# Products of normed rows from layer 1 on as fp16 pairs, with a scale measured for each weight matrix

## The chip, the cores and the metric

One core of a Trainium2 chip runs the whole program. The metric is the device time of one execution in microseconds. The 3 executions of the kernel before took 3876.66 to 3880.73 us, with a median of 3877.01 us.

## What is computed

Two blocks of two layers each work on 512 rows ("latent" tokens) of 1024 features; in the first block 256 context rows go along. Cut to what matters:

```python
# first block, layers l = 0, 1 (context rows get an output in layer 0 only)
u  = modulate(rms_norm(h, g_norm1[l]), shift1, scale1)       # "normed rows"
p  = u @ w_in[l]                 # 1024 x 2720: queries, keys, values of three attentions
g  = sigmoid(u @ w_gate[l] + b_gate[l])                      # 1024 x 3072
h  = h + m2 * (sum(g * (ys @ w_branch[l])) @ w_o[l])
u2 = modulate(rms_norm(h, g_norm2[l]), shift2, scale2)
h  = h + m5 * ((silu(gate) * val) @ w_down[l])               # gate, val = dwconv(u2 @ w_up[l]), 1024 x 5632
# second block, layers l = 0, 1
p  = rmsnorm(x, attn_norm_w[l]) @ w_in_2[l]                  # 1024 x 2964: SSD, short conv, sparse attention
x  = x + concat(y_ssd, y_sc, y_nsa) @ w_out_2[l]
x  = x + (silu(gate) * val) @ ffn_w_down_2[l]                # gate, val = dwconv(rmsnorm(x, .) @ ffn_w_up_2[l]), 1024 x 5504
```

Everything is float32 in memory. The kernel makes each float32 product from two-part operands: with hi = the rounded value and lo = the rest, it adds hi·hi, hi·lo and lo·hi.

## The kernel before

Features lie on the 128 partitions, so a row block of 1024 features is 8 tiles of 128 x 512 (latent) and 8 of 128 x 256 (context). A product with 128 columns of a weight matrix is `mm3`: for each of the 8 feature tiles `wh·uh` and `wh·ul`, then for each `wl·uh`, 24 products into one PSUM bank, each with its own weight load. Both parts of both operands are float32r tiles (4 bytes). `Norm.scale` writes the two parts of the normed rows (`uh`, `ul`: 16 buffers of tag U); `WS.get` loads a block of weights of 256 columns (SyncE's queue, 2 buffers of tag wr) and splits 128 columns of it at a time: ScalarE writes `wh` (128 x 1024), VectorE, or GpSimd where `g.wpool` is set, writes `wl`; 3 buffers each.

The stages follow each other: first block layer 0 (mixer, FFN), layer 1 (mixer, FFN), second block layer 0 and layer 1 (mixer, FFN each). The mixers weave score, softmax and value steps of the heads with products of `w_in`, `w_gate` and others as filling (`weave`, `Fill`). `ffn` goes in chunks of 4 tiles of 128 inner columns: `up` makes gate and value tiles (two products of 24, each evicted by `conv_tile`: one ScalarE and two VectorE instructions that read PSUM), `down` adds the chunk's product to all 8 tiles of `h` (12 products each, evicted by VectorE). During the FFN the generator `ahead` prepares the next layer's parameters. `consumer` is the norm at the end of the FFN: it runs tile by tile behind the last `down`.

The program is written in Tile: a scheduler sets the order on each engine by the order of the program and a model of durations, and hands out buffers of a tag as they come free; engines then run their queues in order. `issue_after(x)` puts an instruction behind `x` on x's engine. K is the tag of wide work tiles: 14 of them in the first block, 22 in the second. PSUM has 8 banks, handed out by tags pM, pT, po, pS; `g.banks` is the list from which `dense` takes its bank in turn. In the second block's mixers it is `["pM"]` (2 banks), and `g.wpool = 1` sends every `wl` of these mixers to GpSimd.

Of the kernel before, what the change touches and what calls it, by code (L numbers as in the profile page):

```python
# [14 lines left out]
OP = mybir.AluOpType  # L15
# [50 lines left out]
class Gen:  # L66
    def __init__(self, tc, ins, outs, ctx, dbg=None):
# [4 lines left out]
        self.hold = []  # L72
# [55 lines left out]
    def parts(self, n, name):  # L128
# [4 lines left out]
        return out  # L133

# [134 lines left out]

    def stats(self, sq, Dn, ntt, eps=EPS, bank="po", small=False):  # L270
# [100 lines left out]
    def dense_raw(self, wp, x, segs, M=P, r0=0, tag="R"):  # L371
        out = self.slot(tag, "dr")
        for sg in segs:
            ps = yield from self.dense(wp, x, sg, M)
            self.act(out[r0:r0 + M, sg[0]:sg[0] + sg[1]], ps)
        return out
# [81 lines left out]
class Norm:  # L458
    def __init__(self, g, h, n, A, B, parts=THIRDS):
        self.g, self.h, self.n, self.A, self.B = g, h, n, A, B  # L460
        self.u, self.rp, self.acc, self.sq = None, [], {}, {}
        self.tiles = [x for x in parts if x[0] < n]

# [59 lines left out]
    def scale(self, i, ks=range(KD)):  # L523
        g = self.g
        o, w = self.tiles[i]
        if self.u is None:
            self.u = [g.parts(self.n, "u") for _ in self.h]
        rp = self.cols(i)
        for k in ks:
# [40 lines left out]
class Between(Norm):  # L570
    def __init__(self, g, h, g1, f):
# [4 lines left out]
        self.A = [gw]  # L576
        self.rs = g.param([P, 4], name="rsk")
# [74 lines left out]
class WS:  # L652
# [7 lines left out]
    def get(self, c, M):  # L660
# [30 lines left out]
        out.key = (id(self), c)  # L691
        return out
# [235 lines left out]
class First:  # L928
    def __init__(self, g, l, h, ada_next=None):
# [4 lines left out]
        self.nq = T if self.ctxq else S  # L934

# [71 lines left out]
    def win(self, c0, c1, cc=256):  # L1007
        return self.g.wstream(self.g.I["w_in"][self.l], 0, KD, c0, c1, cc)
# [329 lines left out]
    def gates(self):  # L1338
        g = self.g
        wg = g.wstream(g.I["w_gate"][self.l], 0, KD, 0, 3 * D)  # L1340
        self.th = []

        def one(d):
            th = g.slot("L", "th")
            wt = wg.get(d * P, P)
            for o, wd in self.qsegs:
                ps = yield from g.dense(wt, self.u, (o, wd))
                g.act(th[:, o:o + wd], ps, AF.Tanh, scale=0.5, bias=self.hbg[:, d:d + 1])
# [73 lines left out]
    def project(self, merged, sp):  # L1422
# [19 lines left out]
        return h, Norm(g, h, nq, A, B).run(tile, self.qsegs)  # L1442

    def run(self, ahead, consumer):
# [16 lines left out]
        u = ffn(g, u2, h, self.qsegs, I["w_up"][l], I["w_down"][l], D_FF, self.cw, self.cb, (0, 44 // 2), 1,  # L1461
# [6 lines left out]
def conv_tile(g, ps, seg, out, cw, cb, c, lead, M):  # L1468
    o, w = seg
    nt = len(cw)  # L1470
    g.act(out[:M, o:o + w], ps, AF.Identity, scale=cw[lead][:M, c:c + 1], bias=cb[:M, c:c + 1])
    for j in range(nt):
# [5 lines left out]
        g.stt(x, ps[:, a + d:b + d], cw[j][:M, c:c + 1], x, OP.mult, OP.add)  # L1478


def ffn(g, u, h, segs, w_up, w_down, dff, cw, cb, coff, lead, scale, consumer, ahead):
# [3 lines left out]
    wg = g.wstream(w_up, 0, KD, 0, dff)  # L1485
    wv = g.wstream(w_up, 0, KD, dff, 2 * dff)
# [3 lines left out]
    def up(ts):  # L1490
        hs = []
        for p0 in range(0, len(ts), 2):
            pair = ts[p0:p0 + 2]
            gates = []
            for t in pair:
# [3 lines left out]
                for sg in segs:  # L1499
                    conv_tile(g, drain(g.dense(w, u, sg, M)), sg, x, cw, cb, coff[0] + t, lead, M)  # L1500
                g.act(x[:M, :n], x[:M, :n], AF.Silu)
                gates.append(x)
            for t, gt in zip(pair, gates):
# [27 lines left out]
    def rest(c, hs):  # L1531
        tile = down(c, hs)
        for d in range(KD):
            for sg in segs:
                tile(d, sg)
    for c in cs[:-2]:
# [3 lines left out]
    drain(ahead)  # L1540
    out = consumer(h).run(down(cs[-1], b), segs, SPLIT)
# [4 lines left out]
class Second:  # L1546
    def __init__(self, g, l, h):
        self.g, self.l, self.h = g, l, h
        self.ws = {}
# [37 lines left out]
    def win(self, c0, c1):  # L1587
        if (c0, c1) not in self.ws:
            self.ws[c0, c1] = self.g.wstream(self.g.I["w_in_2"][self.l], 0, KD, c0, c1, P)
        return self.ws[c0, c1]  # L1590

    def begin(self):
# [3 lines left out]
        hi, lo = g.t("wh", [P, KD, 44], F32R, "wh"), g.t("wl", [P, KD, 44], F32R, "wl")  # L1596
# [3 lines left out]
        g.split(hi, lo, raw)  # L1600
# [634 lines left out]
```

## Time and profile before

| | us |
|---|---|
| median of 3 executions | 3877.01 |
| the profiled execution, device time | 3866.76 |
| its span, first to last instruction | 3865.0 |
| TensorE busy in it | 3704.6 (96%) |
| VectorE, ScalarE, GpSimd busy | 2458.5, 1794.8, 512.0 |

The stages as the loads of their weights bound them in the trace: first block layer 0 mixer 0 to 822, FFN 822 to 1400; layer 1 mixer 1400 to 2075, FFN 2075 to 2455; second block layer 0 mixer 2455 to 2775, FFN 2775 to 3148; layer 1 mixer 3148 to 3462, FFN 3462 to 3865. A product's busy time holds the way through the array, and neighbours overlap; what counts is the distance of their starts. A row of the timeline that merges x products gives it: the start of the next row less its own start, through x; or, with a length L, (L - one duration) / (x - 1).

### The profile page before, as it was taken

Reading aid. Unit: us, or ns where it says so; the run is one execution under the profiler, and the core shown is the slowest. Engines: PE = TensorE matmul, PEld = TensorE weight load, DVE = VectorE, ACT = ScalarE, POOL = GpSimd, SP = SyncE. Lnnn points to the kernel's source line nnn. Section 1 sums busy time; section 2 is a strip of 40 time slices with the busy share of each in tenths; the row PEclk is TensorE's granted clock in tenths of the full one; section 3 lists DMA queues with packets and bytes.
Section 4 is the critical chain, followed back from the end, with each engine's and each line's share of the span. In section 5 each row is a group of like instructions: output and inputs, shape, how many; then the busy total and the mean of one; then the engine's idle time right before and its main releaser. Section 6 shows DMA issues by size and latency. Waiting matters only on the chain. (4 is left out here: it accounts for less than half of the span.)

```text
span 3865.0 us, 54467 instructions
## 1 busy us (share of the span) xinstructions
PE 3704.6 (96%) x20896; PEld 3078.4 (80%) x20896; DVE 2458.5 (64%) x4270; ACT 1794.8 (46%) x3000; POOL 512.0 (13%) x423
## 2 busy tenths in 40 slices
PE   8999999999999999989999999989999998999999
PEld 6888887888888888867767888767788876778886
DVE  5857676656544467668665555678765567876555
ACT  4646666424333236557654333455543335554333
POOL 2101110221000003121112000234100003410000
PEclk9999999999999999999999999989999998999999
DMA  8636898922222225559993322324433322453231
GB/s 246 145 90 153 180 218 226 244 89 79 88 77 87 72 77 131 118 136 216 232 274 126 110 95 93 94 70 104 113 100 98 96 83 67 99 132 98 88 106 60
DMA packets 692255, 483.96 MB, mean 125 GB/s; under 512 B 345790, under 2 KB 620892, under 8 KB 691996
## 3 DMA queue, kind: packets, MB, share of 16 engines
q1 hardware_dynamic: 686172, 468.33, 45.5%
q0 software_dynamic: 5824, 12.15, 1.6%
q8 instruction: 165, 2.70, 0.3%
q14 instruction: 94, 0.77, 0.1%
HBM read 339.32 MB, written 38.67 MB: 98 GB/s over the span
## 5 line engine op out<-in xcount | busy, mean ns | idle before, releaser
L176 ACT ACTIVATE wh<-w 128x1024 fp32r<-128x1024 f32 (+5 forms) x518 | 503.1, 975 | 720.3 <-PE pM L189 232.3
L179 DVE TENSOR_TENSOR wl<-w,wh 128x1024 fp32r<-128x1024 f32 (+3 forms) x464 | 526.0, 1136 | 359.8 <-ACT wh L176 99.7
L189 PE MATMUL pM<-uh,wh 128*128 128x512 f32 (+5 forms) x1832 | 687.2, 381 | 14.6 <-ACT dr L176 9.4
L189 PE MATMUL pM<-ul,wh 128*128 128x512 f32 (+5 forms) x1832 | 662.4, 375 | 0.0
L189 PE MATMUL pM<-uh,wl 128*128 128x512 f32 (+5 forms) x1832 | 450.0, 373 | 0.0
L189 PEld LDWEIGHTS pM<-uh,wh 128*128 128x128 f32 (+3 forms) x1832 | 352.3, 192 | 79.3 <-ACT dr L176 12.7
L189 PEld LDWEIGHTS pM<-ul,wh 128*128 128x128 f32 (+3 forms) x1832 | 343.4, 191 | 56.7
L189 PEld LDWEIGHTS pM<-uh,wl 128*128 128x128 f32 (+3 forms) x1832 | 327.2, 189 | 56.7
L189 PE MATMUL pT<-uh,wh 128*128 128x512 f32 (+3 forms) x912 | 311.1, 353 | 3.0 <-ACT uh L176 2.3
L189 PE MATMUL pT<-ul,wh 128*128 128x512 f32 (+3 forms) x912 | 298.2, 348 | 0.0
L176 ACT ACTIVATE p<-pS,nb 128x768 f32<-128x768 f32 (+7 forms) x304 | 217.6, 716 | 122.4 <-DVE nb L793 116.8
L793 DVE TENSOR_REDUCE nb<-pS 128x1 f32<-128x768 f32 (+7 forms) x304 | 218.0, 725 | 54.6 <-PE pS L189 52.9
L182 DVE SCALAR_TENSOR_TENSOR hl<-p,sm,hl 128x768 f16<-128x768 f32 (+5 forms) x224 | 174.2, 781 | 71.9 <-ACT hl L176 70.4
L176 ACT ACTIVATE hl<-p,sm 128x768 f16<-128x768 f32 (+5 forms) x224 | 159.9, 719 | 108.5 <-DVE sm L1297 26.2
L185 POOL TENSOR_TENSOR rs<-st,half 128x2 f32<-128x2 f32 (+2 forms) x34 | 32.3, 949 | 1327.8 <-DVE st L512 1148.9
L189 PE MATMUL pT<-uh,wl 128*128 128x512 f32 (+3 forms) x912 | 205.3, 351 | 0.0
L185 POOL TENSOR_TENSOR wl<-w,wh 128x1024 fp32r<-128x1024 f32 (+1 forms) x54 | 129.6, 2404 | 537.6 <-ACT wh L176 421.6
L189 PEld LDWEIGHTS pT<-uh,wh 128*128 128x128 f32 (+2 forms) x912 | 171.4, 188 | 28.8 <-ACT uh L176 4.3
L189 PE MATMUL po<-pt,v 128*128 128x128 f16 (+1 forms) x1656 | 174.8, 250 | 16.6 <-DMA pt<-hl 13.0
L189 PEld LDWEIGHTS pT<-ul,wh 128*128 128x128 f32 (+2 forms) x912 | 166.7, 186 | 22.5
L189 PEld LDWEIGHTS <-v 128*128 128x128 f16 x1656 | 123.3, 101 | 60.9 <-issue 43.8
L189 PEld LDWEIGHTS pT<-uh,wl 128*128 128x128 f32 (+2 forms) x912 | 153.8, 188 | 21.9 <-issue 0.4
(581 smaller groups left out, 7763.0 us busy)
## 6 DMA issues: line engine op xcount, KB each, us to landing
w<-w_up SPq DMA_DIRECT2D x44, 1024.0 KB
aw<-w_ada SPq DMA_DIRECT2D x40, 1024.0 KB
w<-ffn_w_up SPq DMA_DIRECT2D x40, 1024.0 KB
w<-w_in SPq DMA_DIRECT2D x70, 512.0 KB
w<-w_gate SPq DMA_DIRECT2D x24, 1024.0 KB
w<-w_down SPq DMA_DIRECT2D x20, 1024.0 KB
ld<-spill SPq DMA_DIRECT2D x51, 384.0 KB
w<-ffn_w_down SPq DMA_DIRECT2D x16, 1024.0 KB
```

Of the source, the lines that this page charges most:

```text
L176: return self.nc.scalar.activation(out, in_, func, **kw)
L179: return self.nc.vector.tensor_tensor(out, a, b, op=op)
L182: return self.nc.vector.scalar_tensor_tensor(out, a, s, b, op0=op0, op1=op1)
L185: return self.nc.gpsimd.tensor_tensor(out, a, b, op=op)
L189: return self.nc.tensor.matmul(out, l, r, start=start, stop=stop)
L793: nc.vector.tensor_reduce(nb, ps, axis=AX.X, op=OP.max, negate=True)
```

## The change

From layer 1 of the first block on, the products of normed rows (`w_in`, `w_gate`, `w_up` of layer 1; `w_in_2`, `ffn_w_up_2` of both layers of the second block) get both operands as fp16 pairs. As fp16 has a small range, rows and weights are scaled first:

- `Norm.fit` takes the largest gain and shift of the norm and scales both, so that the normed rows fit; `Norm.scale` then writes fp16 parts, and both parts of 512 rows lie in one buffer of tag U.
- `Measure` computes one number per matrix, a bound on its largest element, from sums of squares and squared maxima. For this the matrix is read once more from HBM during the FFN before: pieces of 128 x 494 to 768 numbers in buffers of tag K; of three pieces two are squared and summed by ScalarE and one gets its maximum by VectorE. `next(g.slow)` after each tile of `up` and each of the 8 tiles of `down` works two pieces and issues the loads of the next two; the work is put behind the eviction just issued (`g.tail`). These are 128 pieces in the first FFN, 96 in the second, 136 in the third.
- `WS16` splits weights by ScalarE and VectorE with that scale into fp16 parts (one tile `w2`, printed below as `w_`, of the size of a `wh`; tags wh and wl in turn, so 6 pairs instead of 3). GpSimd splits none of these.
- Evictions multiply by the factor that undoes both scales, most in an instruction that was there. In the second block's mixer `conv_silu` now reads PSUM with its four convolution instructions, where a ScalarE copy to SBUF stood ahead; `g.banks` is there `MB`, pM, pT, pM.

```diff
@@ parts
+    def parts16(self, n, name):
+        lat = self.t("U", [P, S], F32, name).bitcast(F16)
+        if n == S:
+            return [lat[:, :S], lat[:, S:]]
@@ dense_raw
-            self.act(out[r0:r0 + M, sg[0]:sg[0] + sg[1]], ps)
+            o = out[r0:r0 + M, sg[0]:sg[0] + sg[1]]
+            self.tail[0] = self.act(o, ps) if f is None else self.act(o, ps, AF.Copy, scale=f[:M])
+class Measure:
+    def behind(self, e, f):
+            if g.tail[e] is not None:
+                st.enter_context(g.tc.issue_after(g.tail[e].ins))
+            f()
+    def steps(self):
+        cols = -(-self.n // width)
+        w = -(-self.n // cols)
+        cuts = [(k, c, min(c + w, self.n)) for k in range(KD) for c in range(0, self.n, w)]
+        def square(i, x):
+            g.act(x, x, AF.Square, accum_out=acc[:, i:i + 1])
+        def largest(i, x):
+            nc.vector.tensor_reduce(a, x, axis=AX.X, op=OP.max, apply_absolute_value=True)
+            g.tt(a, a, a, OP.mult)
+        for i, (k, a, b) in enumerate(cuts):
+            x = g.slot("K", "wm")[:, :b - a]
+            nc.sync.dma_start(x, self.w[k * P:(k + 1) * P, a:b])
+            todo.append((i, x))
+            if len(todo) == 2 or i == n - 1:
+                yield
+                for j, y in todo:
+                    e = int(j % 3 == 2)
+                    self.behind(e, lambda: (square, largest)[e](j, y))
+class WS16:
+    def split(self, raw, n):
+        pr = g.t("wh" if g.ws % 2 else "wl", [P, 2, KD, n], F16, "w2")
+            g.act(pr[:, 0], raw, AF.Copy, scale=self.m.s)
+            g.stt(pr[:, 1], raw, self.m.s, pr[:, 0], OP.mult, OP.subtract)
@@ ffn
+    wg = g.wstream16(w_up, m, 0, dff) if m else g.wstream(w_up, 0, KD, 0, dff)
+    wv = g.wstream16(w_up, m, dff, 2 * dff) if m else g.wstream(w_up, 0, KD, dff, 2 * dff)
+    for x in cw if m else ():
+        g.nc.vector.tensor_scalar(x, x, m.f, None, op0=OP.mult)
@@ up, twice, and rest
+                next(g.slow, None)
@@ conv_silu
-        ps = yield from g.dense_raw(self.win(c, c + P).get(c, P), self.u, [LAT])
+        ps = yield from g.dense(self.win(c, c + P).get(c, P), self.u, LAT)
@@ Second.run
-        g.wpool = 1
+        g.wpool, g.banks = 1, MB
```

SyncE's queue in the FFN of the first block's layer 1, before, from the first chunk's last loads to the third's (`w_up` and `w_down` are weights, 1 MB a row):

```order
L1889 DMA w_4681_25174<-cmp_v_w_2 128x64
L669 DMA w_21731<-w_up 128x8x256
L669 DMA w_21801<-w_up 128x8x256
L669 DMA w_21879<-w_up 128x8x256
L669 DMA w_21949<-w_up 128x8x256
L669 DMA w_22026<-w_down 128x4x512
```

The same place in the changed program, at the first chunk's `down` (`wm` are the measured pieces, 0.38 MB a row):

```order
L771 DMA wm_22129<-w_in 128x741
L771 DMA wm_22154<-w_in 128x741
L812 DMA w_22306<-w_up 128x8x256
L771 DMA wm_22156<-w_in 128x741
L771 DMA wm_22175<-w_in 128x741
L771 DMA wm_22177<-w_in 128x741
L771 DMA wm_22199<-w_in 128x741
L812 DMA w_22396<-w_up 128x8x256
```

Between two loads of weights there now stand four loads of pieces, each of which needs a K buffer that an earlier piece has left, and more of them stand ahead.

ScalarE at the same place before: it splits the next chunk's weights while TensorE is in `down`, then evicts the first gate tile (`gt<-po`):

```order
L176 ACTIVATE wh_22161<-w_22159 128x1024
L176 ACTIVATE wh_22195<-w_22159 128x1024
L176 ACTIVATE wh_22231<-w_22229 128x1024
L176 ACTIVATE wh_22269<-w_22229 128x1024
L176 ACTIVATE gt_22158<-po_22165,cwb_10141,cwa_10134 128x512
```

And in the changed program (`w_4158` and the like are fp16 pairs, `wsc` holds the measured scale, `wss` takes the sums):

```order
L184 ACTIVATE w_4158_22227<-w_22225,wsc_12308 128x1024
L184 ACTIVATE w_4163_22267<-w_22225,wsc_12308 128x1024
L184 ACTIVATE wm_22107,wss_21904<-wm_22107 128x741
L184 ACTIVATE wm_22109,wss_21904<-wm_22109 128x741
L184 ACTIVATE wm_22129,wss_21904<-wm_22129 128x741
L184 ACTIVATE wm_22154,wss_21904<-wm_22154 128x741
L184 ACTIVATE w_4169_22308<-w_22306,wsc_12308 128x1024
L184 ACTIVATE w_4176_22352<-w_22306,wsc_12308 128x1024
L184 ACTIVATE wm_22175,wss_21904<-wm_22175 128x741
L184 ACTIVATE wm_22177,wss_21904<-wm_22177 128x741
L184 ACTIVATE gt_22224<-pS_22230,cwb_10141,cwa_10134 128x512
```

The splits of the next weights and the eviction now have six squares between them, and a square that waits for its piece holds up what stands behind it.

VectorE at the start of the second block's first mixer, before (convolution from the copy `dr` in SBUF; the low parts `wl` are GpSimd's):

```order
L182 SCALAR_TENSOR_TENSOR xc_24094<-dr_24096,hc_21410,xc_24094 128x509
L1618 TENSOR_SCALAR gates_24031<-gates_24031 128x48
L179 TENSOR_TENSOR dx_24034<-po_24026,dtb_21443 128x32
L182 SCALAR_TENSOR_TENSOR xc_24094<-dr_24096,hc_21410,xc_24094 128x510
L1623 TENSOR_SCALAR dz_24036<-dx_24034 128x32
L182 SCALAR_TENSOR_TENSOR xc_24094<-dr_24096,hc_21410,xc_24094 128x511
```

The same in the changed program (convolution from the banks pT and pM; low parts by VectorE itself):

```order
L190 SCALAR_TENSOR_TENSOR w_4614_25004<-w_25002,wsc_21903,w_4614_25004 128x1024
L190 SCALAR_TENSOR_TENSOR xc_24817<-pT_24650,hc_21829,xc_24817 128x509
L190 SCALAR_TENSOR_TENSOR w_4626_25062<-w_25060,wsc_21903,w_4626_25062 128x1024
L190 SCALAR_TENSOR_TENSOR xc_24817<-pT_24650,hc_21829,xc_24817 128x510
L190 SCALAR_TENSOR_TENSOR xc_24825<-pM_24832,hc_21829,xc_24825 128x509
L1810 TENSOR_SCALAR gates_24754<-gates_24754 128x48
```

VectorE's queue takes the splits in between the convolutions, and a bank stays in use until the last of its convolution instructions.

## Rows read from the trace of the kernel before

**Rows 1.** The page's part 1: busy us, share of the span, instructions of each engine.

```profile
PE 3704.6 (96%) x20896; PEld 3078.4 (80%) x20896; DVE 2458.5 (64%) x4270; ACT 1794.8 (46%) x3000; POOL 512.0 (13%) x423
```

**Rows 2.** Windows by stage: length, busy of PE, PEld, DVE, ACT, POOL, clock, DMA share, GB/s.

```profile
822.00:1400.00 578.00, 576.10 (x3466) 507.54 (x3466) 304.34 (x471) 191.08 (x257) 12.77 (x15) 0.99 0.24 77
1400.00:2075.00 675.00, 631.68 (x3800) 517.48 (x3800) 463.27 (x835) 372.45 (x630) 126.90 (x117) 0.96 0.73 177
2075.00:2455.00 380.00, 375.06 (x1724) 313.22 (x1723) 222.08 (x301) 148.20 (x192) 8.32 (x10) 0.99 0.30 96
2455.00:2775.00 320.00, 284.98 (x1631) 229.11 (x1630) 237.85 (x472) 166.38 (x340) 108.02 (x67) 0.91 0.40 98
2775.00:3148.00 373.00, 367.96 (x1680) 302.09 (x1680) 217.99 (x302) 141.13 (x185) 5.13 (x6) 0.99 0.30 93
3148.00:3462.00 314.00, 286.11 (x1608) 226.48 (x1607) 232.45 (x450) 161.46 (x330) 99.14 (x59) 0.92 0.39 97
3462.00:3865.00 403.00, 393.21 (x1806) 319.51 (x1804) 229.92 (x316) 156.45 (x213) 6.30 (x8) 0.98 0.28 90
```

**Rows 3.** Timeline of TensorE, equal products merged: start, length, instruction, products.

```profile
1299.84 1.12 PE L189 MATMUL pS<-uh,wl 128*128 128x256 f32 x8
1300.80 0.40 PE L189 MATMUL pM<-uh,wh 128*128 128x512 f32 x1
...
1304.45 1.98 PE L189 MATMUL pM<-uh,wl 128*128 128x512 f32 x8
1306.26 0.28 PE L189 MATMUL pT<-uh,wh 128*128 128x256 f32 x1
...
329.24 1.47 PE L189 MATMUL po<-pt,v 128*128 128x256 f16 x12 [0.89 <-DMA pt<-hl]
```

**Rows 4.** Groups by shape, whole span, products and weight loads: busy us, mean ns.

```profile
L189 PE MATMUL po<-pt,v 128*128 128x256 f16 x760 | 101.2, 276 | 4.1 <-DVE yb L182 2.9 <-DMA pt<-hl 0.9 <-DMA v<-vhl 0.3
...
L189 PEld LDWEIGHTS pM<-uh,wh 128*128 128x128 f32 x1784 | 346.5, 194 | 71.6 <-ACT dr L176 12.7 <-ACT wh L176 2.2 <-ACT uh L176 1.0
...
L189 PEld LDWEIGHTS <-v 128*128 128x128 f16 x1656 | 123.3, 101 | 60.9 <-issue 43.8 <-DMA pt<-hl 4.4 <-DMA v<-vhl 0.7
```

**Rows 5.** Groups by shape, whole span: splits of weights, and scaled splits into fp16.

```profile
L176 ACT ACTIVATE wh<-w 128x1024 fp32r<-128x1024 f32 x438 | 461.5, 1056 | 668.7 <-PE pM L189 209.8 <-PE pT L189 156.1 <-PE po L189 120.6
L179 DVE TENSOR_TENSOR wl<-w,wh 128x1024 fp32r<-128x1024 f32 x394 | 488.2, 1240 | 312.4 <-ACT wh L176 95.0 <-PE pM L189 78.4 <-PE pT L189 65.8
L185 POOL TENSOR_TENSOR wl<-w,wh 128x1024 fp32r<-128x1024 f32 x44 | 108.1, 2462 | 491.5 <-ACT wh L176 421.6 <-PE pM L189 39.3 <-ACT p L176 19.3
L176 ACT ACTIVATE hl<-p,sm 128x768 f16<-128x768 f32 x64 | 59.7, 934 | 32.7 <-issue 14.6 <-DVE sm L1206 10.4 <-ACT p L176 2.9
L176 ACT ACTIVATE hl<-p,sm 128x512 f16<-128x512 f32 x48 | 34.6, 720 | 26.7 <-DVE sm L1297 11.4 <-issue 6.6 <-ACT p L176 3.7
L182 DVE SCALAR_TENSOR_TENSOR hl<-p,sm,hl 128x768 f16<-128x768 f32 x64 | 66.5, 1038 | 28.4 <-ACT hl L176 27.8
L182 DVE SCALAR_TENSOR_TENSOR hl<-p,sm,hl 128x512 f16<-128x512 f32 x48 | 35.8, 747 | 14.1 <-ACT hl L176 13.5
```

**Rows 6.** Groups by shape, whole span: squares, sums read out, a maximum.

```profile
L176 ACT ACTIVATE sq<-h 128x768 f32<-128x768 f32 x22 | 18.6, 844 | 16.9 <-DVE h L182 16.7
L176 ACT ACTIVATION_READ_ACCUMULATOR p<-pS,nb 128x1 f32 x304 | 58.7, 193 | 0.0
L735 DVE TENSOR_REDUCE vm<-dr 64x1 f32<-64x768 f32 x16 | 15.2, 950 | 1.1 <-ACT dr L176 0.6
```

**Rows 7.** Groups of VectorE by shape, whole span: convolution from SBUF and from PSUM.

```profile
L182 DVE SCALAR_TENSOR_TENSOR xc<-dr,hc,xc 128x510 f32<-128x510 f32 x16 | 20.6, 1290 | 0.1
...
L182 DVE SCALAR_TENSOR_TENSOR gt<-pM,cwb,gt 128x511 f32<-128x511 f32 x23 | 17.2, 748 | 0.6
```

**Rows 8.** Waits of TensorE, 2455 to 2690: us in total, times, longest us.

```profile
PE pM L189 <- ACT dr L176: 5.4, 3, 4.9
```

**Rows 9.** A window of 10 us in the first block's layer 1 mixer, columns as in 2.

```profile
1970.00:1980.00 10.00, 9.96 (x64) 7.94 (x62) 9.29 (x20) 7.15 (x15) 0.00 (x0) 1.00 1.13 346
```

More of the change, by code (lines that the diff above doesn't have):

```diff
@@ new lines, with __init__, load, get @@
+class WS16:
+    def __init__(self, g, w, m, c0, c1, cc):
+        self.g, self.w, self.m, self.c1, self.cc = g, w, m, c1, cc
+        self.rawr = self.curr = (0, 0)
+    def load(self, c):
+        g = self.g
+        e = min(c + self.cc, self.c1)
+        self.raw = g.t("wr", [P, KD, e - c], F32, "w")
+        g.last = g.nc.sync.dma_start(self.raw, self.w[:, c:e].rearrange("(k p) n -> p k n", p=P))
+        self.rawr = (c, e)
+    def split(self, raw, n):
+        g = self.g
+        g.ws += 1
+        pr = g.t("wh" if g.ws % 2 else "wl", [P, 2, KD, n], F16, "w2")
+        with ExitStack() as after:
+            g.soft -= 1
+            for x in g.hold if g.soft >= 0 else ():
+                after.enter_context(g.tc.issue_after(x.ins))
+            g.act(pr[:, 0], raw, AF.Copy, scale=self.m.s)
+            g.stt(pr[:, 1], raw, self.m.s, pr[:, 0], OP.mult, OP.subtract)
+        return pr
+    def get(self, c, M):
+        if not (self.curr[0] <= c and c + M <= self.curr[1]):
+            if not (self.rawr[0] <= c < self.rawr[1]):
+                self.load(c)
+            e = min(c + P, self.rawr[1])
+            o = c - self.rawr[0]
+            self.cur, self.curr = self.split(self.raw[:, :, o:o + e - c], e - c), (c, e)
+        return self.pack(self.cur, c - self.curr[0], M, (id(self), c))
+    def pack(self, pr, o, M, key):
+        out = Wt((pr[:, 0, k, o:o + M], pr[:, 1, k, o:o + M]) for k in range(KD))
+        out.key, out.f = key, self.m.f
@@ L1007, in win, with measures, ready @@
     def win(self, c0, c1, cc=256):
-        return self.g.wstream(self.g.I["w_in"][self.l], 0, KD, c0, c1, cc)
+        g, w = self.g, self.g.I["w_in"][self.l]
+        return g.wstream16(w, self.ms["in"], c0, c1, cc) if "in" in self.ms else g.wstream(w, 0, KD, c0, c1, cc)
+    def measures(self, names):
+        g, l, I = self.g, self.l, self.g.I
+        ws = {"in": (I["w_in"], 2720), "gate": (I["w_gate"], 3 * D), "up": (I["w_up"], 2 * D_FF)}
+        for n in names:
+            self.ms[n] = Measure(g, ws[n][0][l], ws[n][1])
+            yield from self.ms[n].steps()
+    def ready(self, inv):
+        g = self.g
+        for n in ("in", "gate"):
+            self.ms[n].factor(inv)
+        f = self.ms["gate"].t[:, 5:6]
+        g.nc.vector.tensor_scalar(f, self.ms["gate"].f, 0.5, None, op0=OP.mult)
+        self.hf = f
     def groups(self, lat):
@@ L1441, in project @@
         A, B = self.mods(2)
-        return h, Norm(g, h, nq, A, B).run(tile, self.qsegs)
+        m = self.ms.get("up")
+        nm = Norm(g, h, nq, A, B, half=bool(m))
+        u = nm.run(tile, self.qsegs)
+        if m:
+            m.factor(nm.inv)
+        return h, u
     def run(self, ahead, consumer):
@@ L1535, in rest @@
                 tile(d, sg)
+            next(g.slow, None)
     for c in cs[:-2]:
@@ L1548, in __init__, with measures, ready @@
         self.g, self.l, self.h = g, l, h
-        self.ws = {}
+        self.ws, self.ms = {}, {}
+    def measures(self):
+        g, l, I = self.g, self.l, self.g.I
+        for n, w, c in (("in", I["w_in_2"], 2964), ("up", I["ffn_w_up_2"], 2 * D_FF_2)):
+            self.ms[n] = Measure(g, w[l], c)
+            yield from self.ms[n].steps()
+    def ready(self, inv):
+        g = self.g
+        self.f = f = self.ms["in"].factor(inv)
+        self.hf = self.ms["in"].t[:, 5:6]
+        g.nc.vector.tensor_scalar(self.hf, f, 0.5, None, op0=OP.mult)
+        for x in self.hcw:
+            g.nc.vector.tensor_scalar(x, x, f, None, op0=OP.mult)
     def params(self):
@@ L2087, in tile @@
             g.tt(h[d][:, o:o + wd], x[:, o:o + wd], ps, OP.add)
[L2088 removed]
+        nm = Norm(g, h, S, [self.gf], None, half=True)
+        u2 = nm.run(tile, [LAT])
+        self.ms["up"].factor(nm.inv)
         for d in range(KD):
             g.dump(f"2hm{l}_{d}", [h[d][:, :S]])
[L2091 removed]
+        u = ffn(g, u2, self.ms["up"], h, [LAT], I["ffn_w_up_2"][l], I["ffn_w_down_2"][l], D_FF_2, self.fw, self.fb, (0, 22), 2, None, consumer, ahead())
         for i in range(KD):
```

131 lines of the change are left out of this document (100 added, 31 removed).

## The prediction

> **What bounds the kernel now.** I read the page's engine shares first, then windows by stage, then the distances of products in the timeline, and last the groups of the work that the change adds. TensorE is busy for 96% of the span [rows 1]. By stages [rows 2] it is busy for 98% or more of each FFN, with VectorE at 53 to 58% and ScalarE at 33 to 39%. The three FFNs behind 2075 us are therefore TensorE's alone. In the second block's two mixers (2455 to 2775, 3148 to 3462) it is busy for 89 to 91%, VectorE for 74%, the granted clock is 0.91 to 0.92 of 2.4 GHz, and short waits in chains of VectorE and ScalarE share the time. The mixer of layer 1 (1400 to 2075) lies between, at 94%.
>
> A float32r product with 512 columns starts every (1306.26 - 1304.45) / 8 = 0.226 us, one with 256 every (1300.80 - 1299.84) / 8 = 0.120 us [rows 3]; an fp16 product with 256 columns, 276 ns long [rows 4], every (1.47 - 0.276) / 11 = 0.109 us [rows 3]. 256 columns at 2.4 GHz are 0.1067 us, so float32r carries some 13 ns beside its columns and fp16 some 2. No fp16 product with 512 columns is in this trace. I bound it by 0.213 + 0.002 = 0.215 us and by the float32r row, 0.226, and take 0.216, next to the fp16 row: the surplus of float32r is about the same 13 ns at 256 and at 512 columns, so it belongs to the product and not to its columns. The loads of weights point the same way, 194 ns for float32r and 101 for fp16 [rows 4].
>
> **The change part by part.**
>
> *Products.* Counted from the loops, 24 products a tile: each of the three later FFNs has 44 tiles of w_up, of which two go in 256-column pieces: 42 x 24 = 1008 products of 512 columns and 96 of 256. Each second-block mixer has 24 tiles, two in pieces: 528 and 96. The mixer of layer 1 has 24 gate tiles and 22 tiles of w_in, two in pieces, less the context rows' halves: 1056 and 408. In all 3024 + 1056 + 1056 = 5136 products save 0.0105 us and 288 + 192 + 408 = 888 save 0.011 us: 54 + 10 = 64 us, if TensorE never waits for more than before. By stage: 11.7 us for each FFN, 6.6 for each second-block mixer, 15.6 for the mixer of layer 1. In the FFNs I take all, 35 us. In the mixers part of the time goes by other engines' chains and some at the lower clock, so I take 60%: 9 us in layer 1's, 4 us in each of the other two.
>
> *Splits of weights.* The scaled split into fp16 is priced by the split of attention weights, which has the same form: ScalarE 934 ns at 768 and 720 at 512 columns, so 934 + 214 = 1148 ns at 1024; VectorE 1038 and 747, so 1329 ns [rows 5]. Today's are 1056 and 1240. That is +0.09 us each for about 230 splits, 20 us on each of two engines over 1800 us in which both have room: nothing in the FFNs. In the second block's mixers 44 splits leave GpSimd (2.46 us each, 108 us) and come to VectorE: 44 x 1.33 = 58 us, 29 us a mixer on top of 238 of 320 [rows 2], which would be 83%. Against this stands what GpSimd's presence costs VectorE: the convolution step of 510 columns from SBUF takes 1290 ns on average where one from PSUM takes 748 [rows 7], 0.54 us x 16 = 9 us for that one step of three, and other VectorE work in those stretches should lose likewise. ScalarE loses 8 copies of about 0.6 us a mixer, and `dense` has two bank tags in place of one, where TensorE waited 5.4 us for ScalarE's copies [rows 8]. Bounds for each mixer, beside the products: 15 us gained (the waits on copies and splits go) to 10 lost (a third of VectorE's 29 us comes to stand in a chain). I take 5 us gained each, 10 in all, since VectorE still has idle time.
>
> *Measuring.* 360 pieces. A square takes 844 ns at 768 columns, with 193 to read the sum out; a maximum 950 ns at 768 [rows 6], about 1.0 with the small product behind it. Narrower pieces I scale by ScalarE's step in rows 5, 214 ns for 256 columns: 0.79 us at 704, 0.62 at 494. The first FFN gets 87 squares of some 0.8 us (0.2 more for the sums) and 41 maxima: 86 us on ScalarE and 42 on VectorE, in 578. The second gets 65 and 31: 64 and 32 us in 380. The third has 136 narrower ones: 74 and 37 us in 373. Added to rows 2 ScalarE comes to 48, 56 and 58%, VectorE to 60, 68 and 69%. TensorE's 12 or 24 products a tile hide them: a tile of w_up takes 24 x 0.216 = 5.2 us, and five or six banks let it run 15 us ahead of a late eviction. What could come through is lateness of loads. The second FFN's 34.7 MB are read in 52 of its 84 calls, the first three chunks and a little (some 200 us): 173 GB/s on top of 96 is 269. In one `down` (8 x 12 x 0.226 = 21.7 us) 16 pieces of 0.38 MB and two or three blocks of weights are due, 8 to 9 MB, 380 GB/s, where the densest window that I show moves 346 [rows 9]. Each such `down` would end 2 to 3 us late, and SyncE's queue holds weights behind pieces. In the third FFN a `down` asks for 16 x 0.253 + 3 = 7 MB, 320 GB/s; in the first (8 x 12 x 0.346 = 33 us) 5.6 + 3 MB, 260. Bounds: nothing, to a quarter of all the measuring time, 335 / 4 = 84 us. I take 2, 6 and 4 us, the end nearer to nothing, since two blocks of weights are in hand and every engine stays below 70% over a stage.
>
> *The rest.* `fit`, the factors and scaled convolution columns are a handful of instructions of a few columns per stage; most have their inputs long before: 1 us in all, at most 5. The factor rides in instructions that stood there. The freed U buffers and the 6 pairs of weights in hand can only give; I count nothing.
>
> **The sum.** 35 + 9 + 8 + 10 - 12 - 1 = 49 us. The profiled execution, 3866.8 us with 1.8 us beside its span, would come to 3818; it lies 10 us below the median of 3877, and the same gain from the median gives **3828 us**.
>
> **The rivals.**
>
> *The mixers come loose.* If GpSimd's splits were what drew out the second block's mixers, each gains 15 us instead of 5 and its products count in full, as do those of layer 1: 64 + 30 - 13 = 81 us, 3796. For it: 1290 against 748 ns [rows 7]. Against: the longest single wait there is 5 us [rows 8].
>
> *The mixers are bound by chains.* The FFNs give 35 - 12, layer 1's mixer 5, and VectorE's 29 us of splits cost each second-block mixer 10: 35 - 12 + 5 - 20 - 1 = 7 us, 3870. For it: VectorE would be at 83% there. Against: GpSimd's share of its slowness goes.
>
> *Measuring stands in front of TensorE (slower).* ScalarE and VectorE take their work in order; a square whose piece has not landed holds the eviction and the split behind it, and SyncE's weights wait behind pieces that wait for K buffers. The place is `down` and the first tiles behind it in the FFN from 2075 us, where 380 GB/s are due. The gain without measuring is 61 us, so it decides from 61 / 335 = 18% of the measuring time in front of TensorE, some 5 us for each of the 12 chunks that measure. At the quarter of the upper bound: 84 - 61 = 23 us lost, 3900. For it: the sums of loads. Against: nothing but weights and evictions of a few us stands behind a piece, and TensorE has its banks and blocks in hand.
>
> *The type does not matter.* Then an fp16 product of 512 columns starts every 0.226 us like today's, the change only reads weights twice, and 10 - 12 - 1 = 3 us are lost: 3880. The rows speak against it, 0.109 against 0.120 us at equal columns [rows 3]. The Trainium skill says just this (TensorE: Matmul & The Clock Gate, section "Weight-path perf modes — Fast Weight Load (FWL) and DoubleRow"): the array takes one element per cell and cycle whatever its width, and a load of weights scales with columns, not bytes. The trace disagrees for the load, 194 against 101 ns [rows 4], and the same section allows a faster load for types other than FP32.
>
> **How the numbers follow.** Forecast 0.62; mixers loose 0.15; mixers bound 0.10; measuring in front 0.08; type of no matter 0.05. A measurement of this kernel tells about 0.2% from no change, 7.8 us, so faster means below 3869 and slower above 3885. Faster: 0.61 + 0.15 + half of 0.10 = 0.81. Same: 0.05 of the bound mixers, 0.04 of the type and 0.01 of the forecast's edge: 0.10. Slower: 0.09. The forecast's own range takes measuring from 0 to 30 us and the mixers from +15 to -5 each: 3796 to 3866 (20 us better, or 18 + 20 worse). Including the loose mixers and most of the bound ones, **3788 to 3870** leaves out about 2 in 10.
>
> **What would show it.** Products of `u` and `w2` starting every 0.216 us, and the FFN from 3462 us (no measuring) shorter by some 12 us, show the first step; 0.226 refutes it and most of the gain. The FFN from 2075 shorter by 6 and the one from 2775 by 8, with no waits of TensorE on splits or weights in `down`, show that measuring is hidden; waits of ScalarE on pieces, followed by waits of TensorE, would show the slower rival. In the second block's mixers convolution steps near 750 ns and VectorE near its 74% show that GpSimd's withdrawal pays for the splits; VectorE above 83% and longer mixers show the chains. I am wrong in sign if the FFNs that measure come out longer than before by more than the later stages save.

## The result, and the profile after

The changed kernel takes 3832.5 us (median of 4 runs, 3831.1 to 3838.2), the kernel before 3876.8 beside it (3869.8 to 3880.7): ratio 0.989, 95% interval 0.9873 to 0.9908. The forecast of 3828 us was 4.5 us below the measured median; its sign and its range held. The steps behind it held less well, and the experiments are about those.

The page's first part after the change, to be read beside [rows 1]:

```profile
PE 3637.8 (95%) x20911; PEld 2597.8 (68%) x20911; DVE 2558.6 (67%) x4651; ACT 1973.0 (52%) x3470; POOL 401.7 (10%) x386
```

TensorE is 67 us less busy, its weight loads 481 us less, GpSimd 110 us less; ScalarE is 178 us busier. The same windows by stage as in [rows 2], with edges at the new stage ends (first: the FFN that measures layer 1; then mixer and FFN of layer 1, and of each second-block layer):

```profile
888.00:1461.00 573.00, 569.77 (x3438) 499.78 (x3438) 351.14 (x592) 264.02 (x436) 13.83 (x18) 0.99 0.48 164
1461.00:2115.00 654.00, 602.75 (x3664) 401.26 (x3661) 453.45 (x819) 370.66 (x614) 122.67 (x113) 0.96 0.73 180
2115.00:2482.00 367.00, 356.23 (x1653) 211.12 (x1652) 257.92 (x397) 199.24 (x325) 17.48 (x18) 0.98 0.58 195
2482.00:2786.00 304.00, 273.26 (x1662) 178.23 (x1661) 230.70 (x493) 157.59 (x319) 41.77 (x37) 0.93 0.38 96
2786.00:3161.00 375.00, 365.62 (x1661) 209.02 (x1659) 253.02 (x416) 197.78 (x371) 5.21 (x8) 0.98 0.60 191
3161.00:3469.00 308.00, 268.15 (x1631) 175.21 (x1630) 219.98 (x476) 157.26 (x318) 43.34 (x37) 0.92 0.37 92
3469.00:3829.00 360.00, 351.76 (x1613) 203.83 (x1611) 207.36 (x265) 142.94 (x188) 1.40 (x2) 1.00 0.29 92
```

The measuring FFNs move 164, 195 and 191 GB/s, where [rows 2] had 77, 96 and 93. The second-block mixers did not come to VectorE's 83%: 231 of 304 and 220 of 308 us. Products and splits, by a timeline of TensorE and by groups (busy us, mean ns):

```profile
2299.76 2.75 PE L197 MATMUL pT<-u,w 128*128 128x512 f16 x12
2302.35 1.03 PE L197 MATMUL pM<-u,w 128*128 128x512 f16 x4
```
```profile
L190 DVE SCALAR_TENSOR_TENSOR w<-w,wsc,w 128x1024 f16<-128x1024 f32 x225 | 290.6, 1307 | 105.1 <-ACT w L184 103.1 <-PE pS L197 1.3
L184 ACT ACTIVATE w<-w,wsc 128x1024 f16<-128x1024 f32 x225 | 251.7, 1143 | 170.1 <-DMA w<-ffn_w_up 53.1 <-DMA w<-w_in 45.8 <-DMA w<-w_gate 17.4
L190 DVE SCALAR_TENSOR_TENSOR xc<-pM,hc,xc 128x510 f32<-128x510 f32 x11 | 8.2, 743 | 0.0
```

Twelve products take 2302.35 - 2299.76 = 2.59 us, 0.216 each, as forecast (float32r 0.226, [rows 3]). The splits take 1.31 and 1.14 us (forecast 1.33 and 1.15), the convolution step 743 ns (forecast 748).

I set a stage's end at the start of the last VectorE step that scales a norm (`ut<-h`), or the span's end. The whole study in these lengths (F1: layer 1 of the first block; N0, N1: layers 0 and 1 of the second block; "two banks" means pM alone), from one profile of each run, with the median of its executions and the ratio of that to the median of the kernel before, run beside it:

| run | F1 mixer | F1 FFN | N0 mixer | N0 FFN | N1 mixer | N1 FFN | median | ratio |
|---|---|---|---|---|---|---|---|---|
| before | 657.7 | 375.2 | 314.0 | 377.3 | 307.4 | 373.3 | 3876.8 | 1 |
| after | 653.4 | 367.3 | 303.8 | 374.9 | 308.1 | 360.4 | 3832.5 | 0.9890 |
| e1 no measuring | 657.3 | 367.0 | 302.4 | 368.7 | 309.9 | 360.4 | 3829.8 | 0.9891 |
| e2 mixer edits, float32r | 657.6 | 374.6 | 307.9 | 378.5 | 298.7 | 373.3 | 3854.5 | 0.9954 |
| e3 two banks | 660.5 | 367.6 | 296.2 | 376.6 | 299.0 | 360.4 | 3814.5 | 0.9846 |
| e4 convolution by SBUF | 656.7 | 367.3 | 307.6 | 375.7 | 315.5 | 360.4 | 3838.0 | 0.9915 |
| e5 = e2, two banks | 657.9 | 374.6 | 312.2 | 377.8 | 292.9 | 371.9 | 3850.9 | 0.9952 |
| e6 two products a gate | 640.1 | 367.4 | 301.2 | 374.5 | 311.2 | 360.4 | 3819.9 | 0.9870 |
| e7 third bank pS | 651.4 | 366.7 | 314.5 | 376.8 | 308.8 | 360.4 | 3843.2 | 0.9938 |
| e8 VectorE splits, float32r | 654.6 | 374.6 | 308.1 | 377.9 | 290.0 | 371.8 | 3850.5 | 0.9946 |
| e9 = e8 in fp16 | 657.2 | 366.7 | 306.5 | 375.3 | 297.8 | 360.5 | 3824.3 | 0.9893 |
| e10 = e3, splits held | 654.3 | 362.7 | 297.0 | 373.9 | 289.1 | 360.4 | 3801.3 | 0.9831 |
| e11 = e3, three pairs | 650.4 | 366.3 | 288.8 | 374.1 | 287.6 | 362.7 | 3796.8 | 0.9822 |
| e12 three pairs | 652.2 | 367.5 | 293.3 | 374.4 | 297.5 | 362.7 | 3807.6 | 0.9833 |

The medians of the kernel before beside these runs are 3865.9 to 3876.8 us, so ratios are what compares the runs. How far a single profile can be read: after, e1 and e6 have the same second-block mixers, and their lengths differ by up to 2.6 us (N0) and 3.1 us (N1). F1's mixer in fp16 is the same work in seven profiles (all fp16 rows but e6, and but e11 and e12, whose three pairs hold there too) and ranges from 651.4 to 660.5. Differences within these spreads are read as nothing.

By stage the change brought: F1's mixer 4.3 us (forecast 9), its FFN 7.9 (11.7 - 6), N0's mixer 10.2 and N1's -0.7 (9 each), N0's FFN 2.4 (11.7 - 4), N1's FFN 12.9 (11.7), and the FFN that only measures 0.2 (-2). These add up to 37 us and not to the 44 of the medians: the profiled execution of the kernel before (3866.8 us) lies 10 us below its median.

### The profile page after: what moved, and what is told of

Its sections match the earlier page's. It is cut to its first block, busy times and chain, and to the rows that moved or that the text cites. A ratio compares the mean times of both kernels' runs of the same rounds, so it can differ in the third digit from the quotient of the medians.

```text
span 3829.3 us, 55805 instructions
## 1 busy us (share of the span) xinstructions
PE 3637.8 (95%) x20911; PEld 2597.8 (68%) x20911; DVE 2558.6 (67%) x4651; ACT 1973.0 (52%) x3470; POOL 401.7 (10%) x386
## 5 line engine op out<-in xcount | busy, mean ns | idle before, releaser
L197 PEld LDWEIGHTS <-w 128*128 128x128 f16 (+3 forms) x6024 | 585.8, 100 | 646.4 <-issue 70.8
L197 PE MATMUL pM<-u,w 128*128 128x512 f16 (+3 forms) x3000 | 670.4, 374 | 10.1 <-DVE sz L190 2.8
L197 PE MATMUL pT<-u,w 128*128 128x512 f16 (+3 forms) x1968 | 425.3, 364 | 11.1 <-ACT u L184 3.1
L184 ACT ACTIVATE wh<-w 128x1024 fp32r<-128x1024 f32 (+5 forms) x288 | 262.4, 917 | 286.1 <-PE pM L197 85.7
L187 DVE TENSOR_TENSOR wl<-w,wh 128x1024 fp32r<-128x1024 f32 (+5 forms) x278 | 299.2, 1080 | 130.4 <-ACT wh L184 60.4
L190 DVE SCALAR_TENSOR_TENSOR w<-w,wsc,w 128x1024 f16<-128x1024 f32 (+1 forms) x230 | 294.0, 1293 | 105.1 <-ACT w L184 103.1
L184 ACT ACTIVATE w<-w,wsc 128x1024 f16<-128x1024 f32 (+1 forms) x230 | 255.0, 1132 | 170.1 <-DMA w<-ffn_w_up 53.1
L197 PE MATMUL pM<-uh,wh 128*128 128x512 f32 (+2 forms) x720 | 248.1, 357 | 1.6 <-ACT uh L184 0.9
L197 PE MATMUL pM<-ul,wh 128*128 128x512 f32 (+2 forms) x720 | 241.0, 352 | 0.4 <-POOL ul L193 0.4
L184 ACT ACTIVATE wm<-wm 128x501 f32<-128x501 f32 (+6 forms) x243 | 174.7, 721 | 37.1 <-DMA wm<-w_up 11.2
L197 PE MATMUL pS<-kh,qs 128*128 128x256 f32 (+3 forms) x352 | 126.2, 367 | 17.5 <-ACT p L184 15.8
```

The source lines that it names most:

```text
L184: return self.nc.scalar.activation(out, in_, func, **kw)
L187: return self.nc.vector.tensor_tensor(out, a, b, op=op)
L190: return self.nc.vector.scalar_tensor_tensor(out, a, s, b, op0=op0, op1=op1)
L197: return self.nc.tensor.matmul(out, l, r, start=start, stop=stop)
```

## The experiments

Theory at the start: the gain that is missing in two FFNs went into measuring, and the mixers are short of gain because their chains, not their products, end last. The rival: measuring is hidden, and something among the mixers' own edits takes back what the type brings.

**e1, no measuring.**

```
-        for i, (k, a, b) in enumerate(cuts):
...
+        nc.vector.memset(acc[:, :n], 16.0 / n)
```

> The changed kernel without the measured loads, squares and maxima: the sum of squares of each matrix is replaced by a constant (2048), everything else stays, so this run leaves out the measuring of the weights. Theory A (the gain that is missing went into measuring): the three measuring FFNs give back 2, 6 and 4 us as in the sum of the prediction, 3832 - 12 = 3820 us, and the FFN that measures the last second-block layer falls from 374.9 to about 366 us, the length of the other later ones. Theory B (measuring is hidden, the missing gain sits in the mixers' chains): 3832 within 3 us, and every FFN as long as before within 2 us.

3829.8 us (3827.1 to 3831.7), ratio 0.9891 beside 0.9890. Two of the measuring FFNs keep their length within 0.3 us, as theory B has it. N0's is 6.2 us shorter, below all nine fp16 profiles that measure there (373.9 to 376.8), which is nearer to theory A. Its products gain nothing, though: the last VectorE step that adds to `h` starts 353.2 us into this FFN with measuring and 354.4 without. The difference lies behind that step, at the norm's end: 21.8 us with measuring (20.2 to 22.4 in the nine), 14.3 without, 14.6 in the kernel before. A wait of TensorE there in the changed kernel, 2950 to 3161, is gone in e1:

```profile
PE po L197 <- DVE sq L187: 3.3, 1, 3.3
```

So the pieces themselves, 189 us of ScalarE and 93 us of VectorE in the three FFNs, are hidden behind products, and why N0's norm ends later with them stays open. The medians show neither a gain nor a loss. The question moves to the mixers.

**e2, the mixers' other edits under float32r.** In the kernel before:

```
-        ps = yield from g.dense_raw(self.win(c, c + P).get(c, P), self.u, [LAT])
+        ps = yield from g.dense(self.win(c, c + P).get(c, P), self.u, LAT)
...
-        g.wpool = 1
+        g.wpool, g.banks = 1, MB
```

and the streams of w_in_2 split on VectorE always.

> The kernel before with only the three edits of the second-block mixers that have nothing to do with the type: the low halves of the w_in_2 splits on VectorE, the wider rotation of PSUM banks, the convolution read from PSUM. Products stay float32r. Theory A (the relief is worth 5 us in each of the two mixers, as the prediction had it): 3877 - 10 = 3867 us, mixers of 309 and 302 us where before they took 314.0 and 307.4. Theory B (VectorE, which gets 44 splits of 1.2 us, pays for it; what the first of the mixers gained in the changed kernel came from the type): 3877 to 3885 us, no mixer shorter by over 2 us.

The mixers are shorter by 6.1 and 8.7 us: theory A, and more than its 5. But then fp16 with the same edits (after) has an N1 mixer 9.4 us longer than float32r.

**e3 and e4, two of the edits undone in the changed kernel.** e3 sets `g.wpool = 1` and leaves `g.banks` alone (two banks). In e4 ScalarE copies the product to SBUF, and the convolution reads the copy.

> The changed kernel with the two pM banks alone for the products of the second-block mixers, as before the change. Theory A (the wait of products for ScalarE to empty a bank was real, 5.4 us in the first mixer before): each mixer 3 to 5 us longer, 3839 to 3842 us. Theory B (with the shorter products the chains end last and the banks are no matter): 3832 within 3 us.

> The changed kernel with the convolution of the second-block mixers read from an SBUF copy again (16 copies by ScalarE). Theory A (reading PSUM directly is a relief, 0.5 us for each of 48 steps of VectorE when GpSimd is in the way): 2 to 5 us longer in each mixer, 3836 to 3842 us. Theory B (the steps held the PSUM bank while VectorE was behind, which is why the second of the two mixers gained nothing): the second mixer falls from 308 to 303 us, 3827 us.

e3 came out on the side that neither theory had: 7.6 and 9.1 us shorter, and its ratio, 0.9846 (0.9823 to 0.9870), lies just below the interval of the change. The third bank, which I had booked as relief, was a loss. e4 is 3.8 and 7.4 us longer: reading PSUM directly is a relief with three banks.

**e5, e7, e8: banks and splits apart.** e5 is e2 with two banks; e7 is after with `["pM", "pS", "pM"]`; e8 is before with the VectorE splits alone.

> The kernel before, float32r, with the low halves of the w_in_2 splits on VectorE and the convolution read from PSUM, but with the two pM banks as before (the run with all three edits had mixers of 307.9 and 298.7 us and 3854.5 us in all). Theory A (the third bank, taken from the transposes' pT, delays the chains whatever the type): both mixers some 8 us shorter than with it, 300 and 291, 3840 us. Theory B (the third bank hurts only where products are short, under float32r it is the relief that the prediction took it for): 313 and 304 us, 3865 us.

> The changed kernel, in which the third bank of the second-block mixers' products is a score bank (pS, three buffers) in place of pT. Theory A (the loss comes from taking pT from the chains' own transposes): the mixers are as short as with two pM banks, 296 to 299 us, about 3815 us. Theory B (the loss comes from products that run further ahead of the chains, whichever bank they take): 304 and 308 us as in the changed kernel, 3832 us.

> The kernel before, float32r, with one edit: the low halves of the w_in_2 splits on VectorE in place of GpSimd. Theory A (GpSimd beside VectorE was the price: 45 us of slower VectorE steps in the first of the mixers): both mixers 4 to 8 us shorter than 314.0 and 307.4, 3862 to 3869 us. Theory B (44 splits of 1.24 us more on VectorE eat what it gains; the relief is the convolution from PSUM): mixers as long as before within 2 us, 3871 to 3877 us.

Under float32r the third bank does nothing in the sum (e5 to e2: -4.3 and +5.8). pS as third bank is no better than pT (N0 even 10.7 us worse), so sparing the transposes' bank does not undo the loss; whether pS loses for a reason of its own is not shown. Which step the third bank delays I did not isolate. e8 is the largest single effect of the mixers' edits: 5.9 and 17.4 us from one edit, theory A, in N1 beyond its bounds. Its convolution step, still read from SBUF, beside the 1290 ns of [rows 7]:

```profile
L182 DVE SCALAR_TENSOR_TENSOR xc<-dr,hc,xc 128x510 f32<-128x510 f32 x16 | 11.9, 745 | 0.0
```

So 1290 ns was GpSimd's presence and not SBUF's price. It is the step that changed most: the two beside it, of 509 and 511 columns, fell from 945 and 885 ns to 875 and 778. The Trainium skill (SBUF — State Buffer, section "SBUF: two separate sides") states a lock of this kind: VectorE and GpSimd share a port pair that one instruction holds whole, also where a VectorE instruction has two SBUF inputs and GpSimd reads SBUF. The step has two SBUF inputs, and the trace agrees. From e8 to e5, reading PSUM brings nothing more (+4.1, +2.9).

Two things more stand in the traces. GpSimd's slower delivery of `wl` is no rival cause: among TensorE's waits in these two mixers before, none is for GpSimd. And part of N1's 17.4 us is TensorE's own time: with the same products its busy time fell from 280 to 271 us while the granted clock rose from 0.93 to 0.96 of 2.4 GHz (before, then e8; columns as in [rows 2]):

```profile
3184.00:3492.00 308.00, 280.38 (x1631) 228.43 (x1630) 232.58 (x447) 161.57 (x329) 97.06 (x59) 0.93 0.38 93
```
```profile
3181.00:3471.00 290.00, 271.17 (x1627) 221.06 (x1625) 222.21 (x468) 160.97 (x328) 44.98 (x37) 0.96 0.41 99
```

**e6, less TensorE work in F1's mixer.**

```
+            wt.skip = half
...
+        for i in range(0 if skip else n):
```

> The changed kernel, in which the 24 gate tiles of layer 1's mixer leave out the product of the weights' low half (8 of 24 products of 512 columns a tile; this part of the computation is left out, weights are still split): 24 x 8 x 0.216 = 41.5 us of TensorE less. Theory A (that mixer is TensorE's, the 15.6 us of cheaper products were lost in a chance of order): it falls by 35 us or more, from 653 to 661 us to below 622. Theory B (its length is set by the softmax chains of ScalarE and VectorE, which the gate tiles only fill): it falls by less than half of that, 635 to 650 us.

The mixer takes 640.1 us; against the mean of the seven profiles, 655.8, 41.5 us of products are worth 15.7, 38%. That is theory B's range. In this window of e6 TensorE is busy for 89%, after the change 92%:

```profile
1462.00:2102.00 640.00, 570.14 (x3469) 386.66 (x3467) 450.11 (x817) 369.13 (x613) 125.42 (x112) 0.94 0.77 184
```

The wait that is largest in sum before, and after the change (waits of TensorE: us in total, times, longest), is for the softmax of ScalarE:

```profile
PE pS L189 <- ACT p L176: 7.5, 4, 5.7
```
```profile
PE pS L197 <- ACT p L184: 13.8, 13, 2.0
```

In e6 that wait is 11.2 us, while all of TensorE's waits in this mixer add up to 42 us before, 51 after and 70 in e6. So cheaper products end in waits, but no single one of them takes the gain.

**e9, the type alone in the second-block mixers.** e8 with fp16 pairs (after without the banks and with the copy).

> The changed kernel without two of its edits in the second-block mixers: two pM banks alone, and the convolution read from an SBUF copy. What is left in those mixers is the float32r run with VectorE splits alone (308.1 and 290.0 us), in fp16. Theory A (the type is worth the 4 us that the prediction gave it in each): 304 and 286 us, about 3814 us in all. Theory B (these mixers are bound by their chains, the type gives nothing in either): 308 and 290 us together within 4 us, about 3822 us.

The mixers take 306.5 and 297.8 us, which is -1.6 and +7.8: by lengths neither theory, in all 3824.3 us and near theory B. Three comparisons with equal edits, float32r to fp16, give e8 to e9 +6.2 in the sum of both mixers, e5 to e3 -9.9, e2 to after +5.3. The type as it stands brings these mixers nothing that the three agree on, though 13 us of products are saved. Something must come with it. (Read from PSUM, with two banks in fp16, the convolution is worth 10.3 us in N0 and -1.2 in N1, e9 to e3.)

The trace of the changed kernel shows a candidate in two places. VectorE at the end of F1's FFN (start, length, instruction, idle before and its end):

```profile
2453.03 0.68 DVE L187 TENSOR_TENSOR sq<-sq,sq 128x512 f32<-128x512 f32 x1
2454.59 1.36 DVE L190 SCALAR_TENSOR_TENSOR w<-w,wsc,w 128x1024 f16<-128x1024 f32 x1 [0.87 <-ACT w L184]
2455.88 0.74 DVE L190 SCALAR_TENSOR_TENSOR h<-pT,mod,h 128x512 f32<-128x512 f32 x1
2456.54 1.09 DVE L187 TENSOR_TENSOR sq<-sq,sq 128x512 f32<-128x512 f32 x1
2457.55 0.86 DVE L190 SCALAR_TENSOR_TENSOR h<-pM,mod,h 128x256 f32<-128x256 f32 x2
2458.33 1.27 DVE L190 SCALAR_TENSOR_TENSOR w<-w,wsc,w 128x1024 f16<-128x1024 f32 x1
2459.53 1.77 DVE L187 TENSOR_TENSOR sq<-sq,sq 128x512 f32<-128x512 f32 x1
2461.63 1.28 DVE L190 SCALAR_TENSOR_TENSOR w<-w,wsc,w 128x1024 f16<-128x1024 f32 x1 [0.34 <-ACT w L184]
```

Splits of the next mixer's weights (`w<-w,wsc,w`) stand between the last squares of the norm, and TensorE waits for the last square, 2440 to 2482:

```profile
PE po L197 <- DVE sq L187: 5.5, 1, 5.5
```

And ScalarE, VectorE and TensorE in N1's mixer, columns as above:

```profile
3313.16 0.19 ACT L184 ACTIVATION_READ_ACCUMULATOR p<-pS,nb 128x1 f32 x1
3315.24 1.15 ACT L184 ACTIVATE w<-w,wsc 128x1024 f16<-128x1024 f32 x1 [1.89 <-DMA w<-w_in]
3316.29 0.46 ACT L184 ACTIVATE p<-pS,nb 128x256 f32<-128x256 f32 x1
3316.65 0.19 ACT L184 ACTIVATION_READ_ACCUMULATOR p<-pS,nb 128x1 f32 x1
3316.74 0.69 ACT L184 ACTIVATE hl<-p,sm 128x128 f16<-128x128 f32 x2
3317.33 1.14 ACT L184 ACTIVATE w<-w,wsc 128x1024 f16<-128x1024 f32 x1
3322.79 0.51 ACT L184 ACTIVATE hl<-p,sm 128x256 f16<-128x256 f32 x1 [4.32 <-DMA pt<-hl]
...
3313.58 0.16 DVE L190 SCALAR_TENSOR_TENSOR sm<-sm,gates 128x1 f32<-128x1 f32 x1
...
3323.33 0.48 DVE L190 SCALAR_TENSOR_TENSOR hl<-p,sm,hl 128x256 f16<-128x256 f32 x1 [3.54 <-ACT hl L184]
3323.73 0.68 DVE L187 TENSOR_TENSOR pc<-po,cmask 128x512 f32<-128x512 f32 x1
...
3324.47 0.58 PE L197 MATMUL po<-mh,xp 128*128 128x256 f32 x1 [5.71 <-DVE pc L187]
...
3334.35 1.91 PE L197 MATMUL pT<-u,w 128*128 128x512 f16 x4
```

A split waits 1.89 us for its load, and softmax steps stand behind it: the halves `hl` of two tiles have their scale (`sm`) by 3313.74 and start at 3316.74. ScalarE then splits the next weights and waits 4.32 us for transposes of such halves, VectorE for ScalarE, and TensorE 5.7 us for the bank that `pc` empties. The two weights split here are wanted by no product before 3334.35, the next of `u` and `w`. They are so early because `split` puts a pair of halves into one buffer and takes `wh` and `wl` in turn: six pairs fit where there were three. Over N1's mixer ScalarE waits for these loads (before, after):

```profile
ACT wh L176 <- DMA w<-w_in: 2.1, 2, 1.7
```
```profile
ACT w L184 <- DMA w<-w_in: 20.8, 10, 3.6
```

New theory: splits that run six ahead stand in front of the chains on ScalarE and VectorE. The rival: an early split does no harm, and the mixers' order is a matter of luck.

**e10, splits held, and e11, three pairs**, both on e3:

```
+        g.soft = 5
```
```
-        pr = g.t("wh" if g.ws % 2 else "wl", [P, 2, KD, n], F16, "w2")
+        pr = g.t("wh", [P, 2, KD, n], F16, "w2")
```

> The run with the two pM banks back (F1's FFN 367.6, N0's 376.6 us, mixers 296.2 and 299.0), and in addition the splits of a second-block mixer's weights behind its first two held until the norm has scaled its first 256 tokens, by the hold that the FFN's first splits already have. Theory A (splits of 1.28 us on VectorE that run ahead among the norm's squares make TensorE wait 5.5 us at the end of F1's FFN and 3.6 at the end of N0's): both FFNs 3 to 6 us shorter, about 3805 us in all. Theory B (the splits are needed at once, and held back they make the mixers start late): the FFNs shorter by as much as the mixers get longer, 3814 us.

> The run with the two pM banks back, in which split fp16 pairs use the three wh buffers alone and not wh and wl in turn: three pairs can be ahead of TensorE as in the kernel before, not six. Theory A (the room for six pairs is what lets splits run into the norm's end): F1's and N0's FFN 3 to 5 us shorter, 3806 us. Theory B (the six pairs carry TensorE over late loads while the next matrix is measured, 5 us and more at the worst): the two measuring FFNs longer by 3 us or more, 3820 us.

e10 takes 3801.3 us; F1's FFN is 4.9 us shorter than in e3, N0's 2.7, and N1's mixer, of which I had expected nothing, 9.9. e11 takes 3796.8 us (3793.6 to 3799.2), where I had expected 3806, but the gain is not where I had expected it: the FFNs give 1.3 and 2.5 us, the mixers 7.4 and 11.4. By ratios e10 and e11 lie some 6 and 9 us below e3, and their intervals (0.9818 to 0.9845, 0.9808 to 0.9835) overlap with that of e3, so these gains by stage rest on one profile of each. In e11 TensorE's wait for the last square at the end of F1's FFN is down to

```profile
PE po L197 <- DVE sq L187: 1.7, 1, 1.7
```

and behind the last step that adds to `h` this FFN now takes 21.1 us where e3 takes 24.3. That it is hardly shorter comes from the products ahead of that step, 345.2 us against 343.3: they pay for the smaller room. The last FFN pays 2.3 us likewise.

**e12, three pairs alone**: the same line in the changed kernel, the third bank left in.

> The changed kernel with one line other: split pairs take the three wh buffers alone, so three and not six can be ahead of TensorE; the third bank pT stays. Theory A (splits running ahead and the third bank are two costs that add: with two banks the mixers are 288.8 and 287.6 us): 296 and 296 us, about 3812 us. Theory B (the third bank hurt only because splits ran ahead with it): 288 and 288 us, about 3797 us. Theory C (the splits are no cause, two banks and three pairs met a lucky order): 304 and 308 us, 3832 us.

e12 takes 3807.6 us, ratio 0.9833 (0.9820 to 0.9847), clear of the changed kernel's interval: some 22 us from one line. The mixers are 10.5 and 10.6 us shorter than after, and ScalarE's wait in N1's mixer is

```profile
ACT w L184 <- DMA w<-w_in: 4.8, 4, 2.8
```

This wait is a sign and not the price. e8, with three pairs, has 11.5 us of it in an N1 mixer of 290.0 us, and e10, with six, 11.8 in one of 289.1:

```profile
ACT wh L176 <- DMA w<-w_in: 11.5, 4, 4.8
```
```profile
ACT w L184 <- DMA w<-w_in: 11.8, 7, 2.7
```

That three pairs shorten both mixers is shown twice, with three banks (e12) and with two (e11), and theory C is out. How the 21 us come about is shown at the places above and not summed up; e10, in which a hold of the first splits alone takes 9.9 us from N1's mixer, leaves room for a part of chance in the order.

By lengths theory A has it: room for six pairs and the third bank are two costs that add (e12 to e11: another 4.5 and 9.9). The medians do not confirm the second one: the ratios of e12 and e11 differ by 0.0011, some 4 us, and their intervals overlap, so that the third bank costs anything beside three pairs is not shown clear of noise.

With three pairs the type is worth 28.7 us in the two mixers with two banks (e5 to e11) and 15.8 with three (e2 to e12). Both are more than the 13 us that the products save, so order or noise has a part in them. The lowest of the runs is e11: ratio 0.9822 (0.9808 to 0.9835), below the kernel before and below the change (0.9873 to 0.9908), and not clear of e10 and e12.

## Why the prediction was right, and where its steps were not

*Products.* An fp16 product starts every 0.216 us, as forecast. The FFN that neither measures nor splits weights for a next mixer gained 12.9 us (forecast 11.7). F1's and N0's gained 8.2 and 8.6 even without measuring (e1). Up to the last step that adds to `h` the changed kernel's F1 FFN took 343.1 us (354.5 before), 11.4 less; what is missing lies behind it, where splits stand among the last squares: with them held the whole FFN takes 362.7 (e10), 12.5 below before.

*Layer 1's mixer.* The share was too high: 60% taken, 38% measured (e6). 38% of 15.6 is 5.9 us; fp16 is 1.1 below float32r in the means (655.8 in seven profiles, 657.0 in four), 4.3 in the profile of after, and with three pairs 5.7 (651.3 in two). With a spread of 9 us none of these is sharp.

*Measuring.* The forecast was 2, 6 and 4 us; e1 says 0, 0 and 6 by stage, and nothing that the medians show. The second term failed: a sum of 380 GB/s over one `down` was not what TensorE waits for. The third came out near its number by another way than the one given: not in a `down` that waits for loads, but behind the last product, at the norm's end. The slower rival is out: the loads doubled, and up to the norm's end no FFN got longer.

*The second block's mixers.* The forecast was 18 us, and 9.5 came, by parts that cancel. VectorE's splits in place of GpSimd's gained 23 us (e8), more than the 10 of the whole relief; the rival in which the mixers come loose had named this. The failing steps are two sentences. The second bank tag was booked among the gains, from one wait of 5.4 us [rows 8]: in fp16 it costs 16.7 us with six pairs (e3; 17 by medians). With three pairs one profile of each says 14.4 (e11 to e12), the medians 4 within noise. And "the 6 pairs of weights in hand can only give; I count nothing": they cost 21 us in the mixers (after to e12; 22 by medians). I had looked at what buffers give TensorE, not at what stands behind an early split on the engines that make it.

So the first step of the sum held, and that the total came within 4.5 us was luck, because errors cancelled: relief by VectorE's splits too small, bank and pairs missing as costs, layer 1's mixer too high, measuring too dear. The rival in which the mixers come loose stood at 81 us of gain (3796 from 3877). With bank and pairs taken back the change gives 69 us: e11's 3796.8 us stand beside 3865.9 for the kernel before.

## What to carry to other kernels

Room to run ahead has a price on an engine that works in order: an operand made 16 us before it is wanted stands in front of a chain that is wanted now, and if its load is late, so is the chain. After a change of type that halves a buffer, set the number of buffers again, and price each small edit of a bundle by itself; here one was worth 23 us, and two cost 17 and 21, each alone. Cheaper products pay in full only in a stage where TensorE ends last.

## What the runs showed of the hardware that was not expected

With 22 splits of 2.46 us a mixer on GpSimd, one of VectorE's steps with two SBUF inputs took 1290 ns, and 745 without them; VectorE takes those splits over and is still busy for less (228 us in N0's mixer in e8, 236 before). And 87 to 99 GB/s more of loads in three FFNs cost TensorE no time up to the norm's end, and none in all that the medians show.
